# Causal attention of the last layer: probabilities divided after the product with the values, and another order of its tiles

## The chip, the cores and the metric

The kernel runs on one core of a Trainium2 chip. The metric is the time of one execution on the device, in microseconds (us), as the median of several runs; less is better.

## The reference, cut to what matters

Three layers follow one another on 512 tokens of width 1024: a layer of pooling and neighbourhood attention, a layer with a recurrent scan, and a last layer, whose mixer is two kinds of causal attention with 8 heads each. Only the last layer's attention is touched.

```python
# first kind: dense causal attention, 8 heads, queries and keys of 96, values of 64
s = einsum('bqhd,bkhd->bhqk', qi, k) * scale
s = where(kpos <= qpos, s, -1e30)
p = softmax(s)
o_mla = einsum('bhqk,bkhd->bqhd', p, v)
...
# second kind: dilated attention, 8 heads of 64, windows (128, 1), (512, 4), (2048, 16)
outs, lses = one banded causal attention for each window and step
w = softmax(stack(lses))
o_dil = sum(w * outs)
...
mix = concatenate([o_mla, o_dil]) @ w_o
x = x + g1 * mix
```

The kernel computes the dilated kind as one causal attention over all keys, with a mask that adds the logarithm of how many of the three windows hold a pair of query and key.

## The kernel before, in words

The program is traced in Python instruction by instruction. A scheduler of the framework (`TileContext(nc, schedule_with_timeline_sim=True)`) then puts each engine's instructions into a fixed order: of those that are ready on its own assumed timeline, the one traced first goes first. It also places the tiles of the pools and adds the semaphores. So the order written in Python is a priority, and neighbouring steps mix.

`stage2` (L1649) is the last layer. It projects the tokens, brings Q and K of both kinds into rows by head (turns of heads at L1771, their copies at L1772; Q's last scaling is L1828) and then closes its inner pools. The attention opens pools in their place: `s2act` with the result of both kinds, split in a high and a low part (c_hi and c_lo, 16 KB a partition each), `s2at` with the tiles of the attention, and `s2am` with the two masks, loaded by SP (L1847). `self.psum` shares the eight PSUM banks among four tags, two each: a for scores, b for transposes, st for the result of a tile, mm for the output product.

Sixteen shapes of work follow in the order of two loops: for i from 0 to 3 (128 queries each), both kinds (0 is the dense one, 1 the dilated one). One call of `causal` (L1909) is a tile of 128 queries and n = (i + 1) x 128 keys, for 8 heads, taken in pairs. For each head it

- multiplies Q with K on PE into a (L1920, 96 rows, for the dense kind; L1923, 64 rows, the upper or the lower half in turn, for the dilated one),
- adds the mask and takes the row maximum on DVE (L1926), negates it (L1927), and takes the exponential with the row sum on ACT (L1928),
- inverts the sum (L1929) and scales the probabilities by it on DVE (L1930).

`pv` (L1233) then transposes the probabilities of both heads in blocks of 128 (L1241, PE, into b), copies them to the tile pT (L1243, by the scheduler's choice on ACT) and multiplies (L1247) with the values as the stationary operand:

```python
for i in range(n):
    for hh in range(2):
        bi = nc.tensor.matmul(out[hh * 64:(hh + 1) * 64], vs[hh][i], pTs[hh][:, i * 128:(i + 1) * 128], start=i == 0, stop=i == n - 1)
```

So two heads write the two halves of the partitions of one bank st, with features on partitions and queries along the row. A product of f32 operands stands in the trace as two matmuls, each with its own load of the stationary operand; a transpose as one. `split_sb` (L594) rounds the tile's result to the high part on ACT (L596) and takes the rest on DVE (L597). At last the output product (`dense`, with `mm3`, L590 to L592) multiplies the weights wo with all eight blocks of c_hi and c_lo over all 512 tokens, the four blocks of the dense kind first, and L1859 adds it to x.

Of the kernel before, what the change touches and what calls it, by code (L numbers as in the profile page):

```python
# [10 lines left out]
F32 = mybir.dt.float32  # L11
# [3 lines left out]
AF = mybir.ActivationFunctionType  # L15
ALU = mybir.AluOpType
# [533 lines left out]
class Prog:  # L550
# [1098 lines left out]
    def stage2(self, bcs):  # L1649
        tc, nc = self.tc, self.nc  # L1650
        xb = [self.x[:, i, :] for i in range(8)]
        mod = self.mod[2]
        with ExitStack() as ctx:
            E = ctx.enter_context
            p = E(tc.tile_pool(name="s2a", bufs=1))
            QD, KD = p.tile([128, 4, NX], F32, name="QD"), p.tile([128, 4, NX], F32, name="KD")
# [8 lines left out]
            t2 = ctx1.enter_context(tc.tile_pool(name="s2t", bufs=2))  # L1665
            y2 = ctx1.enter_context(tc.tile_pool(name="s2y", bufs=4))
            small, self.small = self.small, ctx1.enter_context(tc.tile_pool(name="s2small", bufs=3))
            with ExitStack() as ctx2:
# [28 lines left out]
                for k in range(8):  # L1697
                    s = slice(k * 32, (k + 1) * 32)
# [18 lines left out]
                for u in (5, 6, 3, 4, 7, 8):  # L1717
                    w = self.wsplit(self.i["win2"][u])
                    v = self.small.tile([128, 16], F32, name="hnv", tag="hnv")
                    ys = []  # L1720
                    for th in range(2):
                        ps = self.pt("mm")
                        for t in range(2):
                            tt = th * 2 + t
                            ts = slice(tt * 128, (tt + 1) * 128)
                            for k in range(8):
                                s = slice(k * 256, (k + 1) * 256)
# [15 lines left out]
                    r = self.rsqrt_small(v, 16)  # L1743
# [19 lines left out]
            Q, K = pb.tile([128, 8, NX], F32, name="Q"), pb.tile([128, 8, NX], F32, name="K")  # L1763
# [10 lines left out]
            with ExitStack() as ctx2:  # L1774
# [4 lines left out]
                v = self.small.tile([128, 32], F32, name="hnk", tag="hnk")  # L1779
                pss = []  # L1780
                for tt in range(4):
                    ps = self.pt("mm")
                    for k in range(2):
                        ts, s = slice(tt * 128, (tt + 1) * 128), slice(k * 512, (k + 1) * 512)
# [4 lines left out]
                for half in range(2):  # L1789
                    vh = v[:, half * 16:half * 16 + 16]  # L1790
                    nc.vector.tensor_scalar(vh, vh, 1.0 / 64, 1e-6, ALU.mult, ALU.add)
                    r = self.rsqrt_small(vh, 16)
# [11 lines left out]
                for u in range(2):  # L1804
                    w = self.wsplit(self.i["wqb"][u], 1536)
                    v = self.small.tile([128, 2, 16], F32, name="hnq", tag="hnq")
# [28 lines left out]
            with ExitStack() as ctx2:  # L1835
                E2 = ctx2.enter_context
                act = E2(tc.tile_pool(name="s2act", bufs=1))
                chi, clo = act.tile([128, 8, NX], F32R, name="c_hi"), act.tile([128, 8, NX], F32R, name="c_lo")
                with ExitStack() as ctx3:
                    t2 = ctx3.enter_context(tc.tile_pool(name="s2at", bufs=2))  # L1840
                    t1 = ctx3.enter_context(tc.tile_pool(name="s2am", bufs=1))
                    self.psum(mm=2, st=2, a=2, b=2)
                    masks = []
                    for n in ("mcaus", "mdil"):
                        o, k = CST[n]
                        t = t1.tile([128, k], F32, name="c_" + n)
                        nc.sync.dma_start(t, self.i["cst"][:, o:o + k])  # L1847
                        masks.append(t)
                    for i in range(4):
                        for kind in range(2):  # L1850
                            self.causal(t2, i, kind, masks[kind], Q, K, vm, QD, KD, vdt, chi, clo)
                self.tap("c_hi", chi.bitcast(F32))
                for u in range(4):
                    w = self.wsplit(self.i["wo2"][u])
                    for m in range(2):
                        ps = self.pt("mm")
                        self.dense(ps, NX, w, 256, m * 128, (chi, clo))
                        b = u * 2 + m
                        nc.vector.scalar_tensor_tensor(xb[b], ps, mod[:, 16 + b, 0:1], xb[b], ALU.mult, ALU.add)  # L1859
# [47 lines left out]
                        nc.sync.dma_start(self.out[b], xb[b])  # L1907

    def causal(self, t2, i, kind, mask, Q, K, vm, QD, KD, vdt, chi, clo):  # L1909
        nc = self.nc  # L1910
        n = (i + 1) * 128
        qs = slice(i * 128, (i + 1) * 128)
        O = self.pt("st")
        v = vm if kind == 0 else vdt
        for hb in range(4):
            es = []
            for h in (hb * 2, hb * 2 + 1):
                S = self.pt("a")
                if kind == 0:
                    nc.tensor.matmul(S[:, :n], Q[0:96, h, qs], K[0:96, h, :n], start=True, stop=True)  # L1920
                else:
                    r = slice((h % 2) * 64, (h % 2) * 64 + 64)
                    nc.tensor.matmul(S[:, :n], QD[r, hb, qs], KD[r, hb, :n], start=True, stop=True)  # L1923
                s = t2.tile([128, 512], F32, name="s", tag="s", bufs=3)
                m = t2.tile([128, 4], F32, name="m", tag="m", bufs=4)
                nc.vector.tensor_tensor_reduce(s[:, :n], S[:, :n], mask[:, 384 - i * 128:512], 1.0, -3e38, ALU.add, ALU.max, m[:, 0:1])  # L1926
                nc.vector.tensor_scalar(m[:, 1:2], m[:, 0:1], -1.0, None, ALU.mult)  # L1927
                nc.scalar.activation(s[:, :n], s[:, :n], AF.Exp, bias=m[:, 1:2], accum_out=m[:, 2:3])  # L1928
                nc.vector.reciprocal(m[:, 3:4], m[:, 2:3])  # L1929
                nc.vector.tensor_scalar(s[:, :n], s[:, :n], m[:, 3:4], None, ALU.mult)  # L1930
                es.append(s[:, :n])
            self.pv(t2, O[:, hb * 128:(hb + 1) * 128], es, [[v[:, k, h * 64:(h + 1) * 64] for k in range(i + 1)] for h in (hb * 2, hb * 2 + 1)])
        kb = slice(kind * 4, kind * 4 + 4)
        self.split_sb(chi[:, kb, qs], clo[:, kb, qs], O.rearrange("p (k t) -> p k t", k=4))


_OUT = ((8, 128, NX), "float32")
# [15 lines left out]
```

## Time and profile before

| what | value |
|---|---|
| median of 3 runs | 3166.5 us (3166.19 to 3166.78) |
| the profiled execution's own time | 3169.68 us |
| its span | 3167.8 us |
| mean granted clock of TensorE | 0.923 |
| PE busy | 2825.9 us (89%) |
| DVE busy | 1786.6 us (56%) |
| ACT busy | 1552.0 us (49%) |
| POOL busy | 1138.5 us (36%) |

Times in the rows are microseconds from the start of the span. PE is TensorE's matmul, PEld its loading of the stationary operand, DVE is VectorE, ACT ScalarE, POOL GpSimd, SP the engine that issues the loads. PEclk is the clock granted to TensorE as a share of 2.4 GHz; it has two levels here, 0.50 (1.2 GHz) and 1.00. A matmul's record covers its whole way through the array, and records overlap, so the pace is read from the distance between starts or from a group's length. A few matmul records can be missing.

### The profile page before, as it was taken

Reading aid. Unit: us, or ns where it says so; the run is one execution under the profiler, and the core shown is the slowest. Engines: PE = TensorE matmul, PEld = TensorE weight load, DVE = VectorE, ACT = ScalarE, POOL = GpSimd, SP = SyncE. Lnnn points to the kernel's source line nnn. Section 1 sums busy time; section 2 is a strip of 40 time slices with the busy share of each in tenths; the row PEclk is TensorE's granted clock in tenths of the full one; section 3 lists DMA queues with packets and bytes.
Section 4 is the critical chain, followed back from the end, with each engine's and each line's share of the span. In section 5 each row is a group of like instructions: output and inputs, shape, how many; then the busy total and the mean of one; then the engine's idle time right before and its main releaser. Section 6 shows DMA issues by size and latency. Waiting matters only on the chain.

```text
span 3167.8 us, 50960 instructions
## 1 busy us (share of the span) xinstructions
PE 2825.9 (89%) x19290; PEld 2343.8 (74%) x19290; DVE 1786.6 (56%) x3557; ACT 1552.0 (49%) x3104; POOL 1138.5 (36%) x1500
## 2 busy tenths in 40 slices
PE   6999889999996899886777769699997999989999
PEld 6967778888885688764666658577876885678887
DVE  8466383444448725758688732644456654556364
ACT  3246556666664633554566532455543444544341
POOL 4013436667675212045666640245543110010000
PEclk9989989999998899987688879799998996999999
DMA  5323213333331565432223231244541220022222
GB/s 224 127 82 98 104 50 128 117 126 127 113 114 61 190 194 156 162 123 84 73 96 103 79 113 53 99 171 170 179 150 56 80 87 7 14 80 90 103 96 85
DMA packets 137589, 345.69 MB, mean 109 GB/s; under 512 B 16385, under 2 KB 48769, under 8 KB 120065
## 3 DMA queue, kind: packets, MB, share of 16 engines
q1 hardware_dynamic: 137344, 342.43, 31.6%
q8 instruction: 153, 2.51, 0.3%
q14 instruction: 92, 0.75, 0.1%
HBM read 293.35 MB, written 49.02 MB: 108 GB/s over the span
## 4 chain that ended last, share of the span: by engine, by line
PE 34%; DVE 8%; ACT 6%; POOL 5%; DMA 4%; issue 2%; SPq 0%; ACTq 0%; POOLq 0%; DVEq 0%
PE mm L590 7%; PE mm L591 7%; PE mm L592 7%; POOL acc L733 2%; DMA adaw<-in_ada_dram 2%; PE a L1288 2%; ACT wh L583 1%; PE st L1247 1%; PE a L329 1%; POOL M L428 1%; POOL Mt L427 1%; PE y L520 1%; DVE G L387 1%; PE a L1920 1%; PE a L1923 1%
## 5 line engine op out<-in xcount | busy, mean ns | idle before, releaser
L733 POOL TENSOR_TENSOR acc<-acc,adat 128x256 f32<-128x256 f32 x658 | 574.9, 896 | 539.2 <-ACT acc L729 434.0
L584 DVE TENSOR_TENSOR wl<-wr,wh 128x2048 fp32r<-128x2048 f32 (+3 forms) x145 | 317.6, 2190 | 361.1 <-ACT wh L583 358.7
L732 ACT ACTIVATE adat<-adaw,silu 128x256 f32<-128x256 f32 x644 | 319.4, 508 | 262.9 <-POOL acc L733 164.0
L583 ACT CAST wh<-wr 128x2048 fp32r<-128x2048 f32 (+2 forms) x147 | 266.8, 1815 | 232.1 <-PE mm L591 218.7
L590 PE MATMUL mm<-fh,wh 128*128 128x512 f32 (+1 forms) x1008 | 350.2, 356 | 14.0 <-DVE relu L1015 9.8
L591 PE MATMUL mm<-fl,wh 128*128 128x512 f32 (+1 forms) x1008 | 353.1, 352 | 2.2 <-DVE fl L597 2.2
L592 PE MATMUL mm<-fh,wl 128*128 128x512 f32 (+1 forms) x1008 | 352.0, 351 | 0.9 <-DVE wl L584 0.9
L590 PE MATMUL mm<-h_xhi,wh 128*128 128x512 f32 (+1 forms) x784 | 277.7, 359 | 3.6 <-ACT h_xhi L596 2.5
L591 PE MATMUL mm<-h_xlo,wh 128*128 128x512 f32 (+1 forms) x784 | 278.2, 357 | 1.8 <-DVE h_xlo L686 1.5
L592 PE MATMUL mm<-h_xhi,wl 128*128 128x512 f32 (+1 forms) x784 | 278.1, 357 | 0.0
L664 POOL TENSOR_TENSOR acc<-acc,t 128x256 f32<-128x256 f32 x127 | 109.1, 867 | 345.0 <-ACT t L662 342.2
L590 PEld LDWEIGHTS mm<-fh,wh 128*128 128x128 f32 x1008 | 192.1, 191 | 42.1 <-DVE relu L1015 12.1
L591 PEld LDWEIGHTS mm<-fl,wh 128*128 128x128 f32 x1008 | 191.7, 190 | 27.6 <-DVE fl L597 4.0
L592 PEld LDWEIGHTS mm<-fh,wl 128*128 128x128 f32 x1008 | 192.0, 191 | 26.2 <-DVE wl L584 1.1
L1039 DVE TENSOR_TENSOR y<-mm,y 128x512 f32<-128x512 f32 (+1 forms) x184 | 99.5, 559 | 152.1 <-PE mm L592 151.6
L590 PE MATMUL mm<-h_hi,wh 128*128 128x512 f32 (+1 forms) x408 | 160.7, 398 | 6.3 <-ACT h_hi L685 6.3
L592 PEld LDWEIGHTS mm<-h_xhi,wl 128*128 128x128 f32 x784 | 149.0, 190 | 21.4 <-issue 0.2
L590 PEld LDWEIGHTS mm<-h_xhi,wh 128*128 128x128 f32 x784 | 147.6, 190 | 23.3 <-ACT h_xhi L596 2.8
L591 PEld LDWEIGHTS mm<-h_xlo,wh 128*128 128x128 f32 x784 | 148.9, 191 | 20.8 <-DVE h_xlo L686 1.7
L427 POOL TENSOR_TENSOR Mt<-M 128x30 f32<-128x30 f32 (+14 forms) x240 | 141.7, 591 | 58.1 <-PE f L443 23.6
L591 PE MATMUL mm<-h_lo,wh 128*128 128x512 f32 (+1 forms) x408 | 160.3, 394 | 0.0
L592 PE MATMUL mm<-h_hi,wl 128*128 128x512 f32 (+1 forms) x408 | 159.6, 393 | 0.0
(451 smaller groups left out, 6929.6 us busy)
## 6 DMA issues: line engine op xcount, KB each, us to landing
adaw<-in_ada_dram SPq DMA_DIRECT2D x256, 256.0 KB, 2.7
wr<-in_w_dram SPq DMA_DIRECT2D x64, 1024.0 KB, 4.8
wr<-in_wup_dram SPq DMA_DIRECT2D x22, 1024.0 KB, 4.7
base<-b SPq DMA_DIRECT2D x32, 384.0 KB, 3.1
ZU<-vt SPq DMA_DIRECT2D x192, 64.0 KB, 2.5
wr<-in_wdn_dram SPq DMA_DIRECT2D x16, 704.0 KB, 4.1
wr<-in_win_dram SPq DMA_DIRECT2D x9, 1024.0 KB, 4.7
wr<-in_evin_dram SPq DMA_DIRECT2D x8, 1024.0 KB, 4.8
```

The costliest lines, as they stand in the source:

```text
L329: nc.tensor.matmul(ps[:, c], bk[g][:, c0 + c].rearrange("p a t -> p (a t)"), G[:, :na, c0 + c, :], start=True, stop=True)
L427: nc.gpsimd.tensor_tensor(t, a, b, ALU.mult)
L583: nc.scalar.copy(hi[:, :n], raw[:, :n])
L584: (eng or nc.vector).tensor_tensor(lo[:, :n], raw[:, :n], hi[:, :n], ALU.subtract)
L590: mm(out, lhs[0], rhs[0], start=first, stop=False)
L591: mm(out, lhs[0], rhs[1], start=False, stop=False)
L592: return mm(out, lhs[1], rhs[0], start=False, stop=last)
L664: nc.gpsimd.tensor_tensor(acc, acc, sq, ALU.add)
L732: nc.scalar.activation(t, w, AF.Copy, scale=s)
L733: nc.gpsimd.tensor_tensor(acc, acc, t, ALU.add)
L1039: nc.vector.tensor_tensor(yb, ps[:, :n], yb, ALU.add)
L1288: bi = nc.tensor.matmul(ps[:, :256], wcol(m, k), z[:, k, o], start=k == 0, stop=k == early - 1)
```

## The change

The two loops change places and run backwards: the dilated kind first, and in each kind the tile with the most keys first. The PSUM pools are allocated in another order. Heads are taken one by one. The mask reduction negates: it computes the mask minus the scores, reduced by the minimum, so that its result is the negated maximum at once, and the exponential takes the scale -1. The probabilities are not scaled; they are transposed, copied on DVE or ACT in turn, and become the stationary operand of the product with the values, so that O holds queries on partitions and 64 columns for each head. The tile o then takes O times the inverse sums, four transposes bring it back to features on partitions, and the split reads those.

```diff
--- before.py
+++ after.py
@@ -1839,15 +1839,15 @@
                 with ExitStack() as ctx3:
                     t2 = ctx3.enter_context(tc.tile_pool(name="s2at", bufs=2))
                     t1 = ctx3.enter_context(tc.tile_pool(name="s2am", bufs=1))
-                    self.psum(mm=2, st=2, a=2, b=2)
+                    self.psum(b=2, st=2, a=2, mm=2)
                     masks = []
                     for n in ("mcaus", "mdil"):
                         o, k = CST[n]
                         t = t1.tile([128, k], F32, name="c_" + n)
                         nc.sync.dma_start(t, self.i["cst"][:, o:o + k])
                         masks.append(t)
-                    for i in range(4):
-                        for kind in range(2):
+                    for kind in (1, 0):
+                        for i in (3, 2, 1, 0):
                             self.causal(t2, i, kind, masks[kind], Q, K, vm, QD, KD, vdt, chi, clo)
                 self.tap("c_hi", chi.bitcast(F32))
                 for u in range(4):
@@ -1907,31 +1907,39 @@
                         nc.sync.dma_start(self.out[b], xb[b])
 
     def causal(self, t2, i, kind, mask, Q, K, vm, QD, KD, vdt, chi, clo):
+
         nc = self.nc
         n = (i + 1) * 128
         qs = slice(i * 128, (i + 1) * 128)
         O = self.pt("st")
         v = vm if kind == 0 else vdt
-        for hb in range(4):
-            es = []
-            for h in (hb * 2, hb * 2 + 1):
-                S = self.pt("a")
-                if kind == 0:
-                    nc.tensor.matmul(S[:, :n], Q[0:96, h, qs], K[0:96, h, :n], start=True, stop=True)
-                else:
-                    r = slice((h % 2) * 64, (h % 2) * 64 + 64)
-                    nc.tensor.matmul(S[:, :n], QD[r, hb, qs], KD[r, hb, :n], start=True, stop=True)
-                s = t2.tile([128, 512], F32, name="s", tag="s", bufs=3)
-                m = t2.tile([128, 4], F32, name="m", tag="m", bufs=4)
-                nc.vector.tensor_tensor_reduce(s[:, :n], S[:, :n], mask[:, 384 - i * 128:512], 1.0, -3e38, ALU.add, ALU.max, m[:, 0:1])
-                nc.vector.tensor_scalar(m[:, 1:2], m[:, 0:1], -1.0, None, ALU.mult)
-                nc.scalar.activation(s[:, :n], s[:, :n], AF.Exp, bias=m[:, 1:2], accum_out=m[:, 2:3])
-                nc.vector.reciprocal(m[:, 3:4], m[:, 2:3])
-                nc.vector.tensor_scalar(s[:, :n], s[:, :n], m[:, 3:4], None, ALU.mult)
-                es.append(s[:, :n])
-            self.pv(t2, O[:, hb * 128:(hb + 1) * 128], es, [[v[:, k, h * 64:(h + 1) * 64] for k in range(i + 1)] for h in (hb * 2, hb * 2 + 1)])
+        m = t2.tile([128, 4, 8], F32, name="m", tag="m", bufs=3)
+        for h in range(8):
+            S = self.pt("a")
+            if kind == 0:
+                nc.tensor.matmul(S[:, :n], Q[0:96, h, qs], K[0:96, h, :n], start=True, stop=True)
+            else:
+                r = slice((h % 2) * 64, (h % 2) * 64 + 64)
+                nc.tensor.matmul(S[:, :n], QD[r, h // 2, qs], KD[r, h // 2, :n], start=True, stop=True)
+            s = t2.tile([128, 512], F32, name="s", tag="s", bufs=3)
+            nc.vector.tensor_tensor_reduce(s[:, :n], S[:, :n], mask[:, 384 - i * 128:512], -1.0, 3e38, ALU.add, ALU.min, m[:, 1, h:h + 1])
+            nc.scalar.activation(s[:, :n], s[:, :n], AF.Exp, bias=m[:, 1, h:h + 1], scale=-1.0, accum_out=m[:, 2, h:h + 1])
+            pt = self.pt("b")
+            for k in range(i + 1):
+                nc.tensor.transpose(pt[:, k * 128:(k + 1) * 128], s[:, k * 128:(k + 1) * 128], self.cst("ident"))
+            pT = t2.tile([128, 512], F32, name="pT", tag="pT", bufs=3)
+            (nc.scalar.copy if h % 2 else nc.vector.tensor_copy)(pT[:, :n], pt[:, :n])
+            for k in range(i + 1):
+                nc.tensor.matmul(O[:, h * 64:(h + 1) * 64], pT[:, k * 128:(k + 1) * 128], v[:, k, h * 64:(h + 1) * 64], start=k == 0, stop=k == i)
+        nc.vector.reciprocal(m[:, 3], m[:, 2])
+        o = t2.tile([128, 512], F32, name="o", tag="o")
+        nc.vector.tensor_tensor(o.rearrange("p (h c) -> p h c", c=64), O.rearrange("p (h c) -> p h c", c=64),
+                                m[:, 3].unsqueeze(2).to_broadcast([128, 8, 64]), ALU.mult)
+        pt = self.pt("b")
+        for k in range(4):
+            nc.tensor.transpose(pt[:, k * 128:(k + 1) * 128], o[:, k * 128:(k + 1) * 128], self.cst("ident"))
         kb = slice(kind * 4, kind * 4 + 4)
-        self.split_sb(chi[:, kb, qs], clo[:, kb, qs], O.rearrange("p (k t) -> p k t", k=4))
+        self.split_sb(chi[:, kb, qs], clo[:, kb, qs], pt.rearrange("p (k t) -> p k t", k=4))
 
 
 _OUT = ((8, 128, NX), "float32")
```

## Rows read from the trace of the kernel before

**Rows 1.** Windows by stage, engines' busy us (instructions), then PEclk, DMA share, GB/s

```profile
2608.80:2612.20 3.40, 3.25 (x16) 2.79 (x15) 2.45 (x13) 2.33 (x5) 0.46 (x1) 0.50 0.76 260
2612.20:2619.10 6.90, 3.65 (x20) 2.05 (x20) 2.17 (x12) 3.88 (x8) 0.00 (x0) 0.99 0.30 103
2619.10:2640.00 20.90, 19.41 (x61) 11.10 (x61) 10.29 (x69) 10.40 (x42) 0.00 (x0) 0.50 0.00 0
2640.00:2680.50 40.50, 39.95 (x124) 21.90 (x124) 16.67 (x86) 16.65 (x54) 0.00 (x0) 0.50 0.00 1
2680.50:2709.00 28.50, 27.21 (x162) 15.14 (x162) 18.50 (x81) 16.82 (x46) 0.00 (x0) 1.00 0.00 1
2709.00:2751.00 42.00, 41.15 (x281) 25.49 (x279) 24.45 (x86) 24.82 (x58) 0.00 (x0) 1.00 0.00 1
2751.00:2789.00 38.00, 37.80 (x165) 31.01 (x166) 12.83 (x11) 10.66 (x18) 13.82 (x12) 1.00 0.24 83
```

**Rows 2.** Groups by line, 2620 to 2751 us: busy us, mean ns, idle before and releasers

```profile
L1241 PE MATMUL b<-cst,s 128*128 128x128 f32 x160 | 33.7, 327 | 0.0
...
L1243 ACT COPY pT<-b 128x128 f32<-128x128 f32 (+3 forms) x64 | 26.5, 423 | 43.2 <-PE b L1241 42.5
L1930 DVE TENSOR_SCALAR s<-s,m 128x256 f32<-128x256 f32 (+3 forms) x63 | 24.2, 386 | 0.8
...
L1929 DVE RECIPROCAL m<-m 128x1 f32<-128x1 f32 x62 | 10.0, 161 | 11.3 <-ACT s L1928 10.8
L1927 DVE TENSOR_SCALAR m<-m 128x1 f32<-128x1 f32 x61 | 8.7, 149 | 0.3
```

**Rows 3.** Chain of waits, narrowest tiles (128 keys): start us, us, what

```profile
2626.59 0.62 PE st L1247 x2
2627.20 0.41 PE b L1241
...
2628.23 0.72 PE a L1923 x2
```

**Rows 4.** Chain of waits, tiles with 384 and 512 keys

```profile
2711.95 0.80 PE st L1247 x10
...
2717.80 0.44 PE b L1241 x4
...
2719.46 0.59 PE b L1241 x4
2720.05 1.02 PE st L1247 x14
...
2722.56 0.86 PE a L1920 x2
2723.78 0.59 PE b L1241 x4
...
2725.97 1.06 PE a L1923 x4
```

**Rows 5.** Waits of SP's queue, 2590 to 2630: us in total, times, longest

```profile
SPq L1847 <- DVE y L1828: 4.9, 1, 4.9
```

**Rows 6.** Timeline of the start of the attention: start us, us, engine, line, operation

```profile
2608.58 1.77 PE L1771 MATMUL t<-cst,y 128*96 128x128 f32 x8 [0.64 <-ACT K L1772]
...
2613.76 0.33 SPq L1847 DMA_DIRECT2D c_mcaus<-in_cst_dram  x1
...
2614.14 0.43 SPq L1847 DMA_DIRECT2D c_mdil<-in_cst_dram  x1
...
2614.82 1.22 PE L1771 MATMUL t<-cst,y 128*96 128x128 f32 x8 [0.66 <-ACT Q L1772]
```

**Rows 7.** Timeline of its end, DVE

```profile
2751.18 0.69 DVE L597 TENSOR_TENSOR c_lo<-st,c_hi 128x512 fp32r<-128x512 f32 x1 [6.31 <-ACT c_hi L596]
```

**Rows 8.** Timeline in the scan layer, PEld: loads for products of two columns

```profile
1614.63 0.97 PEld L530 LDWEIGHTS y<-cst,sq 128*128 128x128 f32 x8
```

**Rows 9.** Window of that stretch, columns as in the first group

```profile
1614.70:1615.50 0.80, 0.80 (x10) 0.80 (x8) 0.80 (x1) 0.78 (x2) 0.00 (x0) 1.00 1.00 384
```

## The prediction

> **What bounds the kernel now.** I read the stage of the causal attention in four steps. First the windows by stage [rows 1]: from 2619 to 2751 us PE is busy for 127.7 of 131.9 us, DVE and ACT for some 70 each, so the stage belongs to PE. The same rows show the price of the stage's first half: from 2619.1 to 2680.5 the granted clock is 0.50 (the 1.2 GHz level), and PE works on the 128- and 256-wide tiles; from 2680.5 on it is 1.00 (2.4 GHz) for the 384- and 512-wide tiles. It had fallen after a stretch in which PE was busy for 3.65 of 6.9 us. Second, the groups by line [rows 2]: 160 transposes (8 heads x 10 key blocks x 2 kinds), all copies of pT on ACT, and 43 us of DVE work for negating, inverting and scaling. Third, the chain of waits [rows 3, 4], which here is PE's own work: it gives the price of each group of matmuls. Fourth, the start and the end of the stage [rows 5 to 7].
>
> **Prices at 2.4 GHz, per 128-key block and head.** Four transposes take 0.44 us where no change of kind of work follows and 0.59 where one does [rows 4]: 0.11 each, and some 0.15 for the change. A 512-wide score product is two passes, 0.86 us: 0.215 per block. The product with the values takes 1.02 us for 14 matmuls and 0.80 for 10: 0.055 each, since two heads write different halves of the partitions and run side by side. Four per block and pair of heads, that is 0.11 per block and head. Together 0.435. A pair of heads takes 4.32 us (from 2719.46 to 2723.78, one transpose group to the one two heads on [rows 4]) where the blocks make 3.48, so the changes cost 0.42 per head. At 1.2 GHz a narrow head takes 0.72 + 0.41 + 0.62 = 1.75 us [rows 3]; twice its blocks (0.22 here for the values, as one head alone has no partner) is 1.09, and 0.66 goes to changes.
>
> **Part 1, the product with the values turned round.** The sums now divide rows of O, so the probabilities must be the stationary operand: 128 x 128 loaded for each pass, and only 64 columns stream. No row before shows that shape. Nearest is the matmul with 128 x 128 f32 weights and two streamed columns [rows 8]: eight loads, each 0.19 long, in 0.97 us, 0.11 apart, at granted clock 1.00 [rows 9]. So loads alone set 0.11 per pass. The lower bound is today's 0.055 per pass, if loads and streams of two heads hid in each other as they do now; the upper is 0.17 (0.11 and the 64 columns' 0.055 one after the other). I take 0.11, the nearest row: 0.22 per block against 0.11, times 160 blocks: **+18 us** (bounds 0 and +35). The Trainium skill (TensorE: Matmul & The Clock Gate, Back-to-back issue gap) has about 81 ns per matmul for a stream of load and matmul pairs with 128 columns, which by itself would make this term about +8 us; the f32 row at 0.11 decides.
>
> **Part 2, heads one by one.** In the widest dilated tile two heads' score products now run side by side in different row halves: 1.06 us for two [rows 4] against 0.86 for one. Emitted singly they lose this: 8 x 0.4, **+3 us**; 0 if the order of PE still puts two together.
>
> **Part 3, transposes of the result.** 8 tiles x 4, 32 x 0.11 and 8 changes at 0.15: **+5 us**.
>
> **Part 4, what goes from DVE and ACT.** 24.2 + 10.0 + 8.7 us of DVE work [rows 2], and half of the 26.5 us of copies moves from ACT to DVE; 8 multiplications of 512 columns (0.69 each, by the 512-wide split of [rows 7]) come. All of it lies beside PE and I cost it at nothing: a 512-wide head will need about 1.1 us of DVE and 1.2 of ACT against 2.6 of PE. If PE stopped being the bound, the 0.16 + 0.49 us of each head's inverse and scaling would be a gain in latency, not in rate. Negating the scores by the scale of the reduction and of the exponential adds no instruction.
>
> **Part 5, the start.** The masks are loaded into space that lies behind the tiles of the attention pool. From the shapes, those take 12.1 KB now and 16.4 KB after (two tiles o, wider m), so the masks slide from over the pools of the small vectors, freed by the last scaling of Q (SP waited 4.9 us for it [rows 5]), to over the pool of Q's last rows, which the last head transposes read. Those run until 2616.04, the loads are issued at 2613.76 and 2614.14 now [rows 6]: 2.3 us later. The dilated mask, needed first, is second in the queue: 0.4 more. SP has nothing else queued behind them that is needed before the stage ends. First waiter is the mask addition on DVE, then the table load and exponential on ACT, then PE: **+2.8 us**, at worst; 0 if the space does not slide. Of that, four score products of the new first tile (1.7 us more than today's narrow four) are done in the wait: **-2**. The new order of the PSUM pools frees the transposes' banks earlier, but the masks come later still: nothing.
>
> **Part 6, the end.** Today the dilated tile is last, and part of the 192 matmuls of the output product (4 x 2 x 8 x 3) runs inside the stage: 165 stand in the stretch after 2751 (last of [rows 1]), and I take 24 as run before. After, the causal kind is last, with which each output product starts, so none can: 24 x 0.23 (37.8 us for 165): **+5.5**. The last tile's multiplication (0.69) and transposes (0.59) come between the last product and the split, handoffs included +1.9: **+2**.
>
> **Part 7, the clock.** 61.4 us run at 0.50 now; at 1.00 the same work is half: **-30.7** if none stays. But the start is as sparse as now, or sparser (PE has only score products between 2616 and the first exponentials, some 6 us), so the clock will be at 1.2 GHz when the 512-wide dilated tile begins. I take 18 us until it rises, since the wide tiles stream long: **+9**. It is 0 if it never falls, and one whole tile, 8 x (4 x 0.55 + 0.42) = 21 us at 2.4 against 8 x (4 x 1.1 + 0.66) = 40, makes +19.
>
> **Sum:** 18 + 3 + 5 + 2.8 - 2 + 5.5 + 2 - 30.7 + 9 = +12.6 us. The profiled execution took 3169.7 (span 3167.8), 3.2 over the median of the runs, 3166.5; I add to the median: **3179 us**. What PE gains by the clock it gives back by loads, side-by-side work and lost filling.
>
> **Rivals.**
> 1. *The order of PE comes out in twos (faster).* If transposes and value products of two heads follow each other, a head has two changes of work instead of three: -0.15 x 64 = -9.6; if dilated score products pair in all tiles: -3 and -0.107 x 48 = -5; if the clock is up at once: -9. All: 12.6 - 26.6 = -14, 3152.5. It decides once more than 19 of the 26.6 us come. For it: PE is the bound and holds two banks for scores and two for transposes, so it will find two heads ready. Against: the narrow tiles show strictly one group after another [rows 3], even though two heads are emitted together there. 0.22, and some part of it, or loads at the lower bound, gives no change (3160 to 3173): 0.17.
> 2. *The clock stays low through the dilated kind.* At 1.2 GHz 8 x (11 + 2.6) = 109 us against 57: +52 in place of +9, 3222. For it: from 2640 to 2680 PE was busy 39.95 of 40.5 us [rows 1] and the clock still was 0.50; now half the PE time is loads with short streams. Against: it rose with the 384-wide tiles. With partial ones (3195 to 3230): 0.13.
> 3. *It never rises before the output products.* 16 x 13.6 + 9 = 227 us of stage, ending near 2849 instead of 2751: +106 with the filling, 3272. A stretch that was mostly head transposes, 2608.8 to 2612.2 at 0.50, was followed by 1.00 [rows 1, 6], so such work can come before a rise: 0.08. The Trainium skill (TensorE: Matmul & The Clock Gate, Part 4) says the opposite: transposes don't count as PE work for the clock, and by that rule this would be the case, as the transposes rise from 160 to 192; the rows here speak against it.
>
> **How the numbers follow.** Forecast (3173 to 3195) 0.40, rival 1 0.22, no change 0.17, rival 2 0.13, rival 3 0.08. A difference under 0.2% (6.3 us) is about what can't be told from none here. Faster 0.22, same 0.17, slower 0.61. The range leaves out rival 3 and the outer half of rival 1: 3153 to 3230; the forecast's own is 3173 to 3195.
>
> **What would show it.** Loads of pT about 0.11 us apart at clock 1.00 (0.055 would take 18 us off); score products of the dilated kind alone or in pairs; the mask loads issued near 2616; a clock of 0.50 at the first tile, and when it rises; no output products before the last tile is done. The forecast is wrong if the clock never falls with the transposes in twos, or if it falls again in the narrow tiles that close each kind.

## The result, and the profile after

The changed kernel takes 3194.7 us (median of 4 runs, 3191.4 to 3199.0) beside 3166.6 for the kernel before (4 runs): a ratio of 1.0074, 95% interval 1.0056 to 1.0092. It is slower by 28 us; the forecast was 12.6. The profiled execution took 3192.2 (span 3190.4).

In this execution the stages ahead were shorter: Q's last scaling (L1828) ends at 2605.12 us, not at 2613.67. 4 of the 8.6 us came between 180 and 200 us, in work that the change doesn't touch, where the clock stood at 0.50 for 10 us instead of 20. Another 3.6 come in the last 85 us before that scaling and belong to the new order. Two dilated heads' scores now run 36 us ahead of the scaling, PE then waits for DVE for 0.44 us where it waited for 2.44, and a stretch of 3.4 us at 0.50 behind that wait is gone. First two lines of after, then one of before, from the timelines:

```profile
2568.85 1.13 PE L1923 MATMUL a<-KD,QD 64*128 64x512 f32 x4
2572.01 0.47 PE L590 MATMUL mm<-wh,kvh 128*128 128x512 f32 x1 [0.44 <-DVE y L1795]
```

```profile
2577.62 0.47 PE L590 MATMUL mm<-wh,kvh 128*128 128x512 f32 x1 [2.44 <-DVE y L1795]
```

All kernels below that open with the dilated kind have this: 80.6 to 80.7 us from the last split of kv on DVE (L597) to Q's last scaling, against 84.0 to 85.4 where the dense kind opens.

I measure from the end of that scaling to the end of the output product (eight tiles, not sixteen: four widths, two kinds): 176.2 us before, 207.5 after, **+31.3**. With the 3.6 us ahead taken off, some 28 are left, which is what the medians show. It splits at the first transpose of probabilities and at the end of the last product with the values: +2.9 for the start (6.8 to 9.7 us), +19.2 for the attention (130.1 to 149.3), +9.2 for the output product (39.3 to 48.5).

Windows of the kernel after, cut where the granted clock or the kind of work changes (columns as in [rows 1]):

```profile
2604.10:2610.90 6.80, 2.74 (x18) 1.57 (x16) 1.02 (x4) 3.43 (x6) 0.00 (x0) 1.00 0.36 128
2610.90:2614.80 3.90, 2.59 (x4) 1.00 (x4) 1.79 (x5) 2.53 (x4) 0.00 (x0) 0.50 0.00 0
2614.80:2640.00 25.20, 25.20 (x79) 16.16 (x78) 6.46 (x18) 7.50 (x19) 0.00 (x0) 0.50 0.00 0
2640.00:2680.00 40.00, 39.28 (x124) 26.01 (x124) 9.49 (x28) 9.73 (x26) 0.00 (x0) 0.50 0.00 1
2680.00:2713.30 33.30, 31.48 (x109) 21.80 (x109) 10.79 (x43) 11.13 (x37) 0.00 (x0) 0.50 0.00 1
2713.30:2764.50 51.20, 46.52 (x322) 38.08 (x320) 27.92 (x91) 28.16 (x83) 0.00 (x0) 1.00 0.00 1
2764.50:2771.30 6.80, 5.73 (x15) 4.32 (x16) 1.03 (x2) 0.58 (x1) 0.00 (x0) 0.50 0.00 0
```

The figure behind the last bracket is PEclk. It falls after a stretch in which PE was busy for 2.74 of 6.80 us, and stays at 0.50 for 102.4 us, the whole dilated kind, although PE is then busy nearly without a break: 25.20 of 25.20 us at first. It rises at 2713.3, just behind the first dense score products, and falls once more when the last tile ends. Before, 61.4 us of the attention stood at 0.50 [rows 1].

Chain of waits of the kernel after (start us, us, what): two heads of the widest dilated tile at 0.50, then heads of the widest dense tile at 1.00:

```profile
2616.79 2.00 PE a L1923 x2
2618.79 1.90 PE st L1933 x8
2620.69 0.85 PE b L1929 x4
2621.55 2.00 PE a L1923 x2
...
2721.95 0.44 PE b L1929 x4
2722.39 0.86 PE a L1920 x2
2723.25 0.84 PE st L1933 x8
```

A dilated head takes 4.76 us (from one score product to the next), a dense one at 1.00 2.14, which is the bare sum of its groups (0.44 + 0.86 + 0.84). Beside [rows 4], where transposes took 0.59 if another kind of work followed and 14 products 1.02, nothing is left in the dense kind for a change of work.

Groups by line after, 2611 to 2766.5 us (columns as in [rows 2]): the new value product of both kinds.

```profile
L1933 PE MATMUL st<-vdt,pT 128*128 128x64 f32 x160 | 40.7, 421 | 1.8 <-DVE pT L1931 1.8
...
L1933 PE MATMUL st<-vm,pT 128*128 128x64 f32 x160 | 22.3, 270 | 3.0 <-DVE pT L1931 2.6 <-ACT pT L1931 0.4
```

The same 160 products cost 40.7 us in the dilated kind and 22.3 in the dense one. Nearly all of the difference is the clock: with the masks loaded early (below), where it stays up for most of the dilated kind, those of the dilated kind cost 24.8. Of the 43 us of DVE work that goes [rows 2], 5.5 come back in the multiplications at L1936.

The start, from SP's waits (engine, line, waited for: us, times, longest) and the timeline:

```profile
SPq L1847 <- PE t L1771: 6.7, 1, 6.7
```

```profile
2607.93 0.33 SPq L1847 DMA_DIRECT2D c_mcaus<-in_cst_dram  x1
...
2608.30 0.43 SPq L1847 DMA_DIRECT2D c_mdil<-in_cst_dram  x1
...
2611.45 0.69 DVE L1925 CUSTOM_DVE_ANT_0 s<-a,c_mdil 128x512 f32<-128x512 f32 x1 [6.34 <-DMA c_mdil<-in_cst_dram]
```

SP now waits for PE's last turns of heads (t, L1771), no longer for the scaling [rows 5]. The first mask load goes out 2.81 us after the scaling's end, 0.09 before [rows 6], and DVE waits 6.34 us for the second one.

The end, from the timeline:

```profile
2764.15 0.69 DVE L1936 TENSOR_TENSOR o<-st,m 128x512 f32<-128x512 f32 x1 [0.97 <-PE st L1933]
...
2764.89 1.12 PE L1940 MATMUL b<-cst,o 128*128 128x128 f32 x4 [0.78 <-DVE o L1936]
...
2766.68 1.22 PE L590 MATMUL mm<-c_hi,wh 128*128 128x512 f32 x2 [0.68 <-ACT c_hi L596]
```

PE is idle for 0.78 and 0.68 us around the four transposes, and no output product stands ahead of 2766.68; before, the first came at 2734.96.

One of the four executions of a later kernel (old heads, new order, full rows; in the table of the next section) took 4564.7 us at a mean granted clock of 0.556; it is left out of that kernel's ratio, not of its median.

### The profile page after: what moved, and what is told of

Its sections match the earlier page's. It is cut to its first block, busy times and chain, and to the rows that moved or that the text cites. A ratio compares the mean times of both kernels' runs of the same rounds, so it can differ in the third digit from the quotient of the medians.

```text
span 3190.4 us, 50844 instructions
## 1 busy us (share of the span) xinstructions
PE 2843.0 (89%) x19322; PEld 2372.3 (74%) x19322; DVE 1772.7 (56%) x3413; ACT 1539.8 (48%) x3072; POOL 1139.3 (36%) x1500
## 4 chain that ended last, share of the span: by engine, by line
PE 33%; DVE 8%; ACT 6%; POOL 6%; DMA 4%; issue 2%; SPq 0%; POOLq 0%; DVEq 0%; ACTq 0%
PE mm L590 7%; PE mm L591 7%; PE mm L592 7%; POOL acc L733 3%; DMA adaw<-in_ada_dram 2%; PE st L1933 2%; ACT wh L583 2%; PE a L329 1%; PE a L1288 1%; PE a L1923 1%; POOL M L428 1%; POOL Mt L427 1%; DVE G L387 1%; ACT adat L732 1%; PE y L520 1%
## 5 line engine op out<-in xcount | busy, mean ns | idle before, releaser
L592 PE MATMUL mm<-h_hi,wl 128*128 128x512 f32 (+1 forms) x408 | 159.3, 393 | 0.0
```

The costliest lines, as they stand in the source:

```text
L592: return mm(out, lhs[1], rhs[0], start=False, stop=last)
```

## The experiments

The question: what holds the clock at 0.50 through the dilated kind, and what do the new heads cost without that? The expectations name theories. **A**: single dilated score products, which cover 64 of 128 rows, hold it down. **B**: the new product with the values does. **D**: the order of the tiles does. **C** is, in the first four, that the clock is a side matter and the loss lies in the new work; in the later ones, that the pause before the stage (PE waits for the masks) is the cause.

The table has every kernel. The ratio is to the kernel before on the same chip (3174.8 to 3177.4 us in these runs). "Stage" goes from Q's last scaling to the end of the output product, "at 0.50" is how much of it from the first transpose on had the lower clock, both from the profiled execution.

| kernel | median us | ratio (95%) | stage us | at 0.50 |
|---|---|---|---|---|
| before | 3166.6 | 1 | 176.2 | 60.0 |
| after | 3194.7 | 1.0074 (1.0056 to 1.0092) | 207.5 | 105.3 |
| after, dense kind first | 3174.9 | 0.9990 (0.9976 to 1.0003) | 180.9 | 57.1 |
| before, new order only | 3147.3 | 0.9901 (0.9883 to 0.9919) | 154.3 | 3.6 |
| before, new heads only | 3175.2 | 0.9994 (0.9977 to 1.0011) | 174.8 | 35.1 |
| after, full rows | 3149.0 | 0.9904 (0.9889 to 0.9919) | 159.3 | 15.1 |
| after, masks early | 3152.9 | 0.9932 (0.9916 to 0.9948) | 162.9 | 17.1 |
| after, full rows, masks early | 3144.6 | 0.9904 (0.9890 to 0.9917) | 149.7 | 3.4 |
| the same, dense kind first, tiles 3, 0, 1, 2 | 3153.5 | 0.9928 (0.9913 to 0.9943) | 151.1 | 6.8 |
| old heads, new order, full rows | 3142.3 | 0.9892 (0.9872 to 0.9912) | 151.0 | 0 |
| the same, masks early | 3141.5 | 0.9898 (0.9883 to 0.9913) | 149.2 | 3.4 |
| before, masks early | 3158.9 | 0.9949 (0.9937 to 0.9962) | 162.3 | 34.2 |
| after, half of the value columns | 3195.9 (one run) | none | 210.4 | 115.4 |

The column "stage" holds one execution of each kernel and leaves out the 3.6 us ahead of the scaling, which all kernels with the dilated kind first gain.

### The order of the kinds

```diff
-                    for kind in (1, 0):
+                    for kind in (0, 1):
                         for i in (3, 2, 1, 0):
```

> The changed kernel with one edit: the dense kind first, the dilated one second, the widest tile first in each. Theory A: the loss is the clock, which stayed at 0.50 from 2611 to 2713 us, through the whole dilated kind, and the kind that opens the stage decides how long it stays down, because the dense kind's score products use 96 of 128 rows and those of the dilated kind 64. Then the clock rises within the first dense tile (8 heads, about 40 us at 1.2 GHz, 17 at 2.4), the dilated kind runs at 2.4 GHz in about 55 us instead of 98, and the time is 3150 to 3162 us, below the kernel before. Theory B: it is the new product with the values (loads of 128 columns for 64 streamed ones) that keeps the clock down whichever kind opens; then the dense kind stays at 0.50 for about 100 us, and the time is 3185 to 3205 us. Theory C: the clock is a side matter and the loss is PE's added work; then the order changes only the end (output products can start inside the stage, 5 us less): 3185 to 3192 us.

Measured: 3174.9 us (0.9990), in none of the three ranges. Windows of this kernel: the first dense head; the dense tiles down to 256 keys; the narrowest dense tile and the first dilated scores; the dilated tiles of 512 and 384 keys; the narrower ones.

```profile
2624.10:2630.90 6.80, 6.07 (x13) 3.45 (x14) 3.28 (x9) 4.15 (x9) 0.00 (x0) 0.50 0.00 0
2630.90:2671.90 41.00, 38.07 (x273) 32.10 (x272) 21.39 (x69) 21.72 (x64) 0.00 (x0) 1.00 0.00 1
2671.90:2688.90 17.00, 17.00 (x48) 9.66 (x48) 5.68 (x21) 6.46 (x21) 0.00 (x0) 0.50 0.00 0
2688.90:2726.50 37.60, 36.67 (x226) 26.77 (x225) 16.49 (x46) 15.83 (x41) 0.00 (x0) 1.00 0.00 1
2726.50:2764.00 37.50, 34.21 (x120) 25.24 (x119) 10.68 (x42) 11.06 (x37) 0.00 (x0) 0.50 0.00 0
```

Where the dense kind opens, the clock is back 6.8 us after the fall behind the same kind of pause, and the narrowest dense tile lets it fall. It comes back at 2688.9 behind the scores of two dilated heads that here ran side by side (both in 2.0 us, which one takes elsewhere) and the transposes that followed, just after the first output product, and the wide dilated tiles, half rows and all, run at 1.00 for 37 us: half rows can go with a high clock, so A falls in its plain form. From the dilated tile of 256 keys on it is low again. B loses support: the same value products stand in stretches of both levels.

### One part alone

The kernel before with the loops and the PSUM order of after, the heads unchanged:

```diff
-                    self.psum(mm=2, st=2, a=2, b=2)
+                    self.psum(b=2, st=2, a=2, mm=2)
...
-                    for i in range(4):
-                        for kind in range(2):
+                    for kind in (1, 0):
+                        for i in (3, 2, 1, 0):
```

> The kernel before with the changed loops and PSUM order alone: dilated kind first, widest tiles first; its own heads in pairs and scaled probabilities. Theory A (the opening kind holds the clock down): pairs of dilated heads run side by side in both row halves, so PE's array is fuller than in the changed kernel; the clock rises in the first tiles and the time is 3140 to 3155 us. Theory B (the new product holds it down): the same, below the kernel before, since the old product is back. Theory D (the order by itself holds the clock down, whatever the product): the clock stays at 0.50 through the dilated kind, about 90 us at 1.2 GHz in place of 61 before: 3175 to 3190 us.

and the opposite, the new `causal` in the old loops and PSUM order:

> The changed kernel with the loops and PSUM order of before: queries ascending, both kinds in turn, narrow tiles first. Theory A: the clock is at 0.50 in the narrow tiles as before, some 65 us, and rises when wide dense tiles come; PE then needs about 2.1 us per widest dense head and 2.4 per dilated one at 2.4 GHz, and the time is 3160 to 3175 us, near the kernel before. Theory B: the clock stays at 0.50 to the end of the stage, 200 us or more: 3250 to 3280 us. Theory C (PE's added work alone, 18 us of loads and 5 of transposes on top of the old order): 3185 to 3195 us.

Measured: 0.9901 and 0.9994. Windows and chain of the new order only, its pause and what follows:

```profile
2612.80:2619.70 6.90, 3.73 (x22) 2.22 (x21) 2.64 (x11) 3.75 (x7) 0.00 (x0) 0.99 0.41 132
2619.70:2626.50 6.80, 6.80 (x20) 3.16 (x18) 4.28 (x15) 4.50 (x9) 0.00 (x0) 0.50 0.00 0
```

```profile
2618.80 4.13 PE a L1923 x6
2622.93 1.90 PE b L1241 x8
2624.83 0.62 PE st L1247 x2
```

A window of the new heads only, and a line of its chain in it:

```profile
2620.00:2654.10 34.10, 31.79 (x115) 25.32 (x116) 13.00 (x60) 15.87 (x57) 0.00 (x0) 0.50 0.01 2
```

```profile
2652.22 0.75 PE st L1933 x4
```

The new order is worth 1% by itself: the same kind of pause lets the clock fall, and it is back after 6.8 us, within the widest dilated tile. D falls. Those 6.8 us hold half-row scores and transposes, but only two passes of the old value product; the scores of three heads took 4.13 us, since they partly overlapped. So this run shows a rise behind half-row scores, and hardly one behind the old value products. The new heads alone change nothing that can be measured. Their clock is low for 34 us of narrow tiles, not the 65 that A expected. It rises at 2654.1 behind dense tiles of 256 keys with the new value product among them: that product does not prevent a rise, and B falls. So neither part is slower than before; only both together are.

### Full rows for the dilated scores

Each head's dilated queries get a tile of 128 rows of their own, with zeros in the rows of the other head, so that a score product covers the whole array and gives the same numbers:

```diff
-            QD, KD = p.tile([128, 4, NX], F32, name="QD"), p.tile([128, 4, NX], F32, name="KD")
+            QD, KD = p.tile([128, 8, NX], F32, name="QD"), p.tile([128, 4, NX], F32, name="KD")
+            nc.gpsimd.memset(QD, 0.0)
...
-                                nc.scalar.activation(QD[:, b], ps, AF.Copy, scale=0.125)
+                                for e in range(2):
+                                    r = slice(e * 64, e * 64 + 64)
+                                    nc.scalar.activation(QD[r, b * 2 + e], ps[r], AF.Copy, scale=0.125)
...
-                nc.tensor.matmul(S[:, :n], QD[r, h // 2, qs], KD[r, h // 2, :n], start=True, stop=True)
+                nc.tensor.matmul(S[:, :n], QD[:, h, qs], KD[:, h // 2, :n], start=True, stop=True)
```

> The changed kernel with one edit: each dilated head's queries stand in a tile of 128 rows whose other 64 rows are zero, so that the dilated score product runs over all 128 rows instead of 64; results are the same. It adds 8 KB of space, a clearing on POOL, and four more copies on ACT of 64 rows each. Theory A (the half-row products hold the clock down, and cost a change of work each): the clock rises within the first dilated tile, each change between kinds of work costs nothing visible, the dilated kind takes 50 to 65 us instead of 98, and the time is 3145 to 3165 us. Theory B (the product with the values holds it down): the clock stays at 0.50 through the dilated kind, and only the changes go, about 0.45 us for each of 32 dilated heads: 3178 to 3186 us.

Measured: 0.9904. Windows of this kernel, and its chain in the widest dilated tile:

```profile
2608.90:2615.70 6.80, 3.03 (x21) 1.83 (x20) 1.58 (x6) 3.77 (x6) 0.00 (x0) 1.00 0.43 147
2615.70:2622.50 6.80, 5.04 (x11) 2.87 (x12) 2.38 (x7) 3.61 (x7) 0.00 (x0) 0.50 0.04 14
2622.50:2680.00 57.50, 53.51 (x366) 43.24 (x365) 32.02 (x102) 32.45 (x93) 0.00 (x0) 1.00 0.00 1
```

```profile
2623.66 0.84 PE st L1935 x8
...
2628.78 0.44 PE b L1931 x4
2629.23 0.86 PE a L1925 x2
2630.09 0.84 PE st L1935 x8
```

The same pause (3.03 of 6.80 us) and the same fall, but the clock is back after 6.8 us, with PE busy for only 5.04 of them. But the first value product of the stage starts at 2623.66, after the rise: full-row scores and transposes brought the clock back before the new value product had run at all. What this run shows of that product is that it keeps a high clock for the 57.5 us that follow. The dilated head costs what a dense one costs, 2.14 us.

### The pause taken away

The masks are loaded into the pool that is opened with Q and K, in place of `s2am`:

```diff
             vm = pb.tile([128, 4, 512], F32, name="vm")
+            masks = []
+            for n in ("mcaus", "mdil"):
+                o, k = CST[n]
+                t = pb.tile([128, k], F32, name="c_" + n)
+                nc.sync.dma_start(t, self.i["cst"][:, o:o + k])
+                masks.append(t)
...
-                    t1 = ctx3.enter_context(tc.tile_pool(name="s2am", bufs=1))
```

> The kernel after the change, with both masks loaded into the pool that is opened with Q and K, long before the attention. Nothing else differs. If the clock fell because PE had only single score products to do while it waited for the masks (theory C: the pause), the dilated kind now opens at once, the granted clock stays 1.00 or comes back within 10 us, the stage loses some 45 us and the time is about 3148. If the half-row score products hold the clock down whatever comes before them (theory A), it falls all the same and stays at 0.50 for 90 us or more, only the start's 2 to 4 us are won, and the time is 3188 to 3193.

Measured: 0.9932, 3152.9 us. Windows, and the chain in the widest dilated tile:

```profile
2611.30:2640.00 28.70, 27.51 (x154) 17.50 (x153) 13.73 (x38) 16.49 (x37) 0.00 (x0) 1.00 0.04 15
2640.00:2665.90 25.90, 24.08 (x149) 16.87 (x148) 12.07 (x43) 12.79 (x40) 0.00 (x0) 1.00 0.00 1
2665.90:2676.10 10.20, 10.04 (x29) 6.52 (x30) 4.02 (x19) 4.31 (x16) 0.00 (x0) 0.50 0.00 1
```

```profile
2625.23 1.05 PE a L1922 x2
2626.29 1.03 PE st L1932 x8
2627.32 0.44 PE b L1928 x4
```

The heads, the order and the half rows are those of after, with no output product among them, and the dilated kind runs at 1.00 from its first tile to its narrowest, where it is low for 10.2 us. The first transpose comes 4.1 us after the scaling of Q instead of 9.7. So half rows do not pull a high clock down in the wide tiles. The low 102 us needed both: a pause behind which the clock fell, and a stage opening behind which it did not rise again. The chain gives the other price of the half rows: scores 1.05 and values 1.03 where full rows have 0.86 and 0.84, 0.38 us more for a head.

Both edits together, the fourth cell:

> The kernel after the change with both edits together, full rows for the dilated queries and the masks loaded early; order of tiles as after. The fourth cell beside after (pause, half rows: low for 102 us), full rows alone (pause, full rows: low for 7 us, 3149) and masks early alone (no pause, half rows: low only in the narrow tiles, 3152.9). If each edit removes the same loss (the low clock) and otherwise only its own price, this one gains the pause over full rows alone (5 to 6 us from the last product of the projections to the first transpose) and the changes of kind of work at half-row operands over masks early alone (about 0.3 us in each of 32 dilated heads, 10 us): 3140 to 3145. If the pause was hidden by other work, it stays at 3149.

Measured: 3144.6 us, inside the range expected; its stage is 149.7 us, 9.6 less than with full rows alone, of which 6.5 are the pause (4.1 against 10.6 us to the first transpose). Beside after, the stage is 57.8 us shorter: the masks early alone make 44.6 of that (5.6 of them the start), the full rows on top 13.2. Its windows:

```profile
2613.00:2650.00 37.00, 35.04 (x234) 27.59 (x233) 19.49 (x57) 22.58 (x54) 0.00 (x0) 1.00 0.03 14
2650.00:2718.80 68.80, 61.01 (x425) 50.08 (x424) 38.39 (x133) 39.13 (x121) 0.00 (x0) 1.00 0.00 1
```

The kernel before with the same edit of the masks, and nothing else:

> The kernel before the change with nothing but the masks loaded early. If the pause is what lets the clock fall, and the stage's opening with narrow tiles only fails to raise it again, the 61.4 us at 0.50 shrink to 10 or less: 25 to 30 us less, and some 3 to 5 for the pause itself: 3140 to 3148 beside 3174.8. If the narrow tiles let the clock fall by themselves, as they did in the middle of the stage in the dense-first order, it is at 0.50 for 40 us or more all the same, and only the pause is won: 3168 to 3172.

Measured: 3158.9, between the two. Windows:

```profile
2612.80:2616.20 3.40, 2.25 (x12) 1.08 (x12) 3.21 (x18) 2.73 (x6) 0.00 (x0) 1.00 0.09 36
2616.20:2653.80 37.60, 35.07 (x110) 20.04 (x110) 15.33 (x97) 17.11 (x62) 0.00 (x0) 0.50 0.00 0
```

Where the narrowest tiles open the stage, the clock falls without the wait for the masks (PE is busy for 2.25 of 3.40 us ahead of the fall), but it is back after 37.6 us instead of 61.4. Both the pause and the narrow tiles were in the price of before.

### What sets the pace of the new value product

The kernel after with half of each head's value columns. The other half of the result's columns is left out: the tile o is cleared on POOL, and the multiplication by the inverse sums takes 32 columns a head; these lines of the edit are not shown.

```diff
-                nc.tensor.matmul(O[:, h * 64:(h + 1) * 64], pT[:, k * 128:(k + 1) * 128], v[:, k, h * 64:(h + 1) * 64], start=k == 0, stop=k == i)
+                nc.tensor.matmul(O[:, h * 64:h * 64 + 32], pT[:, k * 128:(k + 1) * 128], v[:, k, h * 64:h * 64 + 32], start=k == 0, stop=k == i)
...
```

> The kernel after the change, with only 32 of each head's 64 value columns streamed in the product with the values; it leaves out the other half of the result's columns (zeros). If loading the 128 x 128 stationary operand sets the pace (term of Part 1: 0.105 us a pass at 2.4 GHz, 0.22 at 1.2), a group of 8 stays at about 0.84 us in the dense kind and 1.76 in the dilated one. If the streamed columns set it, or add to the load, the group of 8 falls by 8 x 32 columns, about 0.1 us at 2.4 GHz and 0.2 at 1.2 for an addition, and to about half if the columns alone set it.

Chain of this kernel, the dense kind at 1.00:

```profile
2726.92 0.81 PE st L1933 x8
2727.74 0.47 PE b L1929 x4
2728.21 0.86 PE a L1920 x2
```

0.81 for eight passes in place of 0.84 with half of the columns, and the transposes behind them 0.47 in place of 0.44: a head takes 2.14 us either way. The loads set the pace, not the columns.

### Versions that might beat both

Full rows, masks early, and the dense kind first, each kind with the tiles in the order 3, 0, 1, 2:

> The kernel after the change with three edits: the dilated queries lie in 128 rows with zeros in the other head's half (full rows), the masks are loaded early, and the kinds go dense first, in each kind the widest tile first and then 128, 256 and 384 keys. Theory A (half-row score products hold the clock down, nothing else does) expects the clock at 1.00 for all but some 10 us of the stage, no pause for the masks, and output products of the dense kind inside the dilated kind: the 3149 of full rows alone, less 2 to 3 for the start, less about 5 for the filled end and 3 for the low stretch at the end: 3137 to 3143. If narrow tiles pull the clock down in this order too, 10 to 20 us more: about 3155.

Measured: 3153.5, outside the first range and near the second, but not for its reason: the clock did stay up (6.8 us low), and 24 of the 192 output products (some 5 us) lie inside the attention again; but its stage is 151.1 us, not less than with the dilated kind first (149.7). The end is 5.5 us shorter (42.1 against 47.6) and the attention 6.9 longer (104.9 against 98.0): work moved forward into a stretch where PE is busy anyway only changes places. And with the dense kind first the 3.5 us ahead of the scaling are lost (84.2 against 80.7). That covers the 4.2 us between the two profiled executions (3147.5 and 3143.4). The profiled one is the fastest of its four, which go up to 3154.8; the rest of the distance between the medians stays open.

The old heads with full rows, and with the masks early too:

> The old heads in pairs (values stationary, probabilities scaled before the product) in the new order of tiles, with full rows for the dilated queries. It stands beside full rows with the new heads (3149.0) and the old heads in the new order (3147.3). If a change of kind of work costs wherever an operand covers half of the array, the dilated score products no longer do, but the value products with their 64-column halves still do: the wide dilated pair loses its row-half partners (0.86 x 2 in place of 1.06) and gains one or two changes of 0.15 a head, about even, 3143 to 3152. If the changes belong to the order of the work and not to the operands, nothing is gained for the lost partners, and the time is about 3150 to 3156.

> The old heads in pairs, in the new order of tiles, with full rows and masks early: the best of the old heads so far (3142.3) without the pause. If the pause costs its own length, 3136 to 3139; if the pause was hidden by other work, 3142.

Measured: 3142.3 and 3141.5. The pause was worth 1.7 us of stage here, not its own length (4.9 against 9.4 us to the first transpose). The old heads (ratio 0.9898) and the new ones (0.9904) under the same conditions have intervals that overlap almost wholly: with the clock up, the form of the heads makes no difference that shows. These versions beat the kernel before by 0.7 to 1.1%.

## Why the prediction was right or wrong

The sign was right, and the time lies inside the range. That it lies in the forecast's own range, 0.3 us under its upper end of 3195, is luck: the two largest errors went in opposite directions and hid each other. Measured from the scaling of Q the sum was +31.3, forecast +12.6: +2.9 against 0.8 at the start, +19.2 against 4.3 (18 + 3 + 5 - 30.7 + 9) in the attention, +9.2 against 7.5 at the end.

- **Part 7, the clock: the step that failed most.** I took 18 us at 0.50 "since the wide tiles stream long". It was the whole dilated kind. The attention with the same heads and no pause takes 110.2 us, 10.2 of them at 0.50; at 1.00 that is some 105, so the low clock cost after about 44 us, where I had +9: 35 too few. I judged a tile by its width; the runs show that it depends on what went before the tile and on what opens the stage. Single half-row scores with the new value products did not bring the clock back in 98 us of attention, though the opening's first two heads' scores overlapped there too. Full-row scores and transposes did, in 6.8 us, and so did the overlapped half-row scores of the order alone. Elsewhere in the attention of these traces every rise stands behind scores on 96 or 128 rows, or behind dilated scores of two heads side by side. No run has single half-row scores with plenty of the old value products after a fall, so whether the half rows alone or the pair of half rows and new value products is the cause is not shown.
- **The changes between kinds of work, the other error.** The prices kept 0.42 us for each head in the new form. In the dense kind nothing of it is left: 2.14 us a head against 2.60 (four blocks of 0.545 and 0.42). In the dilated kind full rows remove it and half rows bring 0.38 back. So it is the price of going between operands that cover half the array and such that cover it whole, not of changing the kind of work. The Trainium skill (TensorEngine Tiling (Array Packing), Key Properties) says that changing the tiling mode drains TensorE; the trace agrees, with 0.19 us for each of the two longer groups of a head. By this, as an estimate, 32 dense heads at 0.42 make 13 of the 20 us by which the rest of the attention undercut the sum (125 forecast without the clock, 105 estimated above from masks early); the other 7 I can't assign.
- **Part 1** was right in size: 0.105 us a pass, loads as the bound. The 81 ns of the Trainium skill (TensorE: Matmul & The Clock Gate, Back-to-back issue gap) isn't reached by these products, which stream 64 columns and not the 128 of that figure. That its +18 then doesn't show, old heads 149.2 and new heads 149.7 us of stage, fits with the changes that the old form's 64-column halves pay: a dense score product behind them takes 1.05 in place of 0.86 (chain of the kernel before, below this list). Two dense heads take 4.32 us in the kernel before [rows 4] and 4.28 after.
- **Parts 2 and 3**: the score products of the wide tiles came singly and a tile's four transposes took 0.44 us where the clock was up, as forecast. **Part 4** held nearly: in the dense kind PE was busy for 46.5 of 51.2 us, some of the gaps waiting for the copies pT on DVE.
- **Part 5**: the masks slid behind the turns of heads, nearly as worked out (2.7 us later by the distance to the scaling, against 2.3 for the issue). The -2 for score products done in the wait did not come: +2.9 where 0.8 was forecast. The weight of this step was in none of its terms, though: the pause, with the opening behind it, set the clock of the next 102 us.
- **Part 6**: no output product before the last tile, as forecast. The end came to 9.2 us, 1.7 over the 7.5: its first ten products run at 0.50, 0.43 us apart in place of 0.23, which is 2 us.
- **Rivals.** The second is what happened: the clock low through the dilated kind. Its +52 for the clock is near the 44; its time of 3222 was too high because it kept the 0.42. I gave it 0.13, on the argument that the clock had risen with 384-wide tiles before; but there dense tiles with 96 rows lay between the dilated ones. The third fell with the dense kind: the clock was at 1.00 through it, transposes and all. With it fell the rule cited there from the Trainium skill (TensorE: Matmul & The Clock Gate, Part 4), as far as it would keep the clock low: the dense kind, 51.2 us at 1.00, has as many transposes as the dilated one.

The dense score product of the kernel before behind a group of value products, from its chain (Part 1):

```profile
2721.06 1.05 PE a L1920 x2
```

## What to carry to other kernels

Ask what a stage's first tiles do to the clock, not only what the stage does on average: taking away a pause of a few microseconds took the ratio from 1.0074 to 0.9932, because what followed kept a high clock but did not regain it. Take the pause away (load early what the opening needs) or open with work that covers the whole array, as far as these runs go; the zero rows that fill the array cost the score product nothing here (0.86 us on 128 rows, as on 96). And before pricing a change of form, separate what a group costs by itself from what it pays for its neighbour: here the neighbour's price decided.

## What the runs showed of the hardware that was not expected

- PE can be busy without a break and stay at the lower clock: 25.20 of 25.20 us in the kernel after. With full rows the clock came back behind a stretch with 5.04 of 6.80 us.
- The same tiles ran at either level for some 50 us and more, by what had gone before: the dilated tiles of 512 to 256 keys at 0.50 after a fall, at 1.00 without one. The tiles of 128 keys let it fall in the dilated kind (masks early, 2665.9 us) and in the dense one (dense kind first, 2671.9 us), though not in every kernel.
- Going between operands on 64 rows and on 128 cost 0.19 us a time at 2.4 GHz; 96 rows beside 128 cost nothing (2.14 us a dense head, the bare sum).
